# Three summed pairs per gate/up block, their shared products a block ahead and combined in PSUM

## The chip, the core and the metric

The kernel runs on one core of a Trainium2 chip. The core has TensorE (PE) for matrix products, VectorE (DVE), ScalarE (ACT) and GpSimd (POOL) for elementwise work, and SyncE (SP), whose queue issues the loads. Data lie in SBUF, matmul results in PSUM, which has eight banks of 128 x 512 float32 here. The metric is the time on the device in microseconds (us); the median of several runs counts.

## The reference

One decoder layer in float32, 256 tokens, width 2048, followed by a norm:

```
u = rmsnorm(h);  proj = u @ w_in            # 2048 x 6144
a recurrence (RG-LRU) and a retention on parts of proj give y
h = h + y @ w_out                           # 2048 x 2048
u = rmsnorm(h)
ff = silu(u @ w_ffn_gate) * (u @ w_ffn_up)  # 2048 x 5632 each
h = h + ff @ w_ffn_down                     # 5632 x 2048
out = rmsnorm(h)
```

The change lies in the line of `ff`, the gate/up stage.

## The kernel before

**Products in three matmuls.** Every float32 operand is split into a rounded high part and a remainder: `split` (L100) has ScalarE cast the source to the high part (L101) and VectorE subtract it from the source (L102). A product of 128x128 with 128x512 then takes three matmuls: high x high, high x low, low x high (L667, L668, L669).

**The gate/up stage.** The 5632 columns are taken in 11 blocks (`NB`) of 512 gate and 512 up columns, the 2048 rows in 8 steps of 256. One step of one block is a `Quad` (L592): four weight tiles of 128x512, b11 and b21 of gate, b12 and b22 of up, loaded from HBM in two halves of 512 KB. The left side, `hh[i]` (a `Left`, L518), holds the activations of the same 256 rows for two groups of 128 tokens: a11, a12 for the first, a21, a22 for the second. The four results of a block, c11 (gate, first tokens), c21 (gate, second), c12 and c22 (up), are summed over the 8 quads.

**Plain and summed quads.** A plain quad makes the eight products of `EIGHT` (L636), 24 matmuls. A quad whose number is in `SUMMED` (L32) makes the seven of `SEVEN` (L640), 21 matmuls, after Strassen and Winograd: VectorE forms t1 = b11 + b12, t2 = t1 + b22, t3 = b12 + b22, t4 = t2 + b21 (L628 to L632), and the matching left sums s1 to s4 are made once per `Left`. The products p1, p5, p6, p7 go to four banks of their own and are summed over the summed quads of the block; the other three go straight into c11, c21 and c12. After the last summed quad `post` (L723) copies p1 out and forms n = p6 - p1, then n - p5, n - p7 and a further difference in SBUF (L729, L706). When c11, c12, c21, c22 have had their last product, four VectorE instructions add these to them (L734, L736). Then come tanh (L710) and two products on VectorE (L711, L712), and two or three steps later eight transposes (`turn`, L714, L719) and two ScalarE copies put the block's result into `ff`.

**Buffers.** Raw weights: 5 tiles of 128x1024 (`raw`; the sums t1 to t4 use the same pool). Split weights: 4 tiles each for high and low (`wh`, `wl`). 58 tiles of 128x512 (`act_tile`) for the rest. PSUM: two pools of four banks, `bank` and `aux`. In `block` (L645) c11 to c22 always come from `aux`, p1 to p7 and the transposes from `bank`.

**Order.** `program` (a list) holds the steps in order: the quads they need and a function that emits the matmuls. The loop at the end emits, ahead of each step, the loads of everything up to three halves past what the step needs (`AHEAD`, L949), each with its sums and splits, then the step, then what `defer` has put off for so many steps (`tick`). The framework's planner takes the emitted order as priority, estimates when each instruction's inputs are there, and fixes an order for each engine; an instruction that is not ready by this estimate lets later ones pass. On the chip each engine follows its fixed order and waits on semaphores. Loads are all issued on SyncE's queue. The time shows no step boundaries on TensorE: matmuls of neighbouring quads are interleaved.

**Around it.** `out_post` (L545) makes each `Left` in the stage before; `norm2` (L566) makes the second norm's scale during block 0; `resid_tok` (L577) transposes the residual during blocks 1 and 2; `load_fw` runs in the last block. The down projection (`down_block`, L761) uses `block` too, in two halves of 22 quads, the last two of each as a tail.

Of the kernel before, what the change touches and what calls it, by code (L numbers as in the profile page):

```python
# [28 lines left out]

SUMMED = (2, 4)  # L32
SUMMED_DOWN = (2, 5, 8, 11, 14)


# [1 line left out]
def tile_hymba_layer(ctx: ExitStack, tc: tile.TileContext, A: dict, out: bass.AP):  # L37
    nc = tc.nc
# [29 lines left out]
    def bank(name):  # L68
        return pmm.tile([P, 512], F32, tag="mm", name=nm(name))
# [30 lines left out]
    def split(dst_h, dst_l, src):  # L100
        act.copy(out=dst_h, in_=src)  # L101
        v.tensor_tensor(out=dst_l, in0=src, in1=dst_h.bitcast(F32), op=ALU.subtract)  # L102

    class Unit:


        def __init__(self, src, pieces=1, before=None, after=None):
            self.src, self.pieces, self.before, self.after = src, pieces, before, after
# [110 lines left out]
    def defer(steps, f):  # L219
        later.append([steps, f])  # L220
# [371 lines left out]
    class Quad:  # L592

        def __init__(self, src, sums, before=None):
            self.src, self.sums, self.before = src, sums, before
# [44 lines left out]
        ("c11", "a12", "b21"), ("c21", "a22", "t4"), ("c12", "s4", "b22"),  # L642
    )

    def block(quads, lefts, post, ps, tail=(), after=None, ordered=False):  # L645
# [12 lines left out]
        def step(i):  # L658
            def run():
                while at[0] < len(todo) and todo[at[0]][0] == i:  # L660
                    m, (_, c, a, b, c0, cw, *q) = at[0], todo[at[0]]
                    if firsts[c] == m:
                        ps[c] = (aux if c in ("c11", "c12", "c21", "c22") else bank)(c)
                    q = q[0] if q else i
                    (ah, al), (bh, bl) = lefts[q][a], (t[:, c0 : c0 + cw] for t in quads[q].parts[b])
                    p, last = ps[c][:, c0 : c0 + cw], lasts[c] == m
                    pe.matmul(p, ah, bh, start=firsts[c] == m, stop=False)  # L667
                    pe.matmul(p, ah, bl, start=False, stop=False)  # L668
                    pe.matmul(p, al, bh, start=False, stop=last)  # L669
                    if last:  # L670
                        post(c)
                    at[0] += 1
                if after:
                    after(i)

            return run

        for i in range(n):
            program.append(([quads[i]], step(i)))
        if tail:  # L680
# [7 lines left out]
    def ffn_block(j):  # L688
        def after(i):
            if j == 0 and i == SUMMED[-1] + 1:  # L690
                norm2()
            if j in (1, 2) and i < 2:
                resid_tok(2 * j - 2 + i)
            if j == NB - 1 and i == 0:
                load_fw()

        ps = {}
        quads = [Quad(A["w_gu"][j * (KT // 2) + i], i in SUMMED) for i in range(KT // 2)]
        block(quads, hh, ffn_post(j, ps), ps, after=after)

    def ffn_post(j, ps):
        part = {}
# [5 lines left out]
        def gated(t):  # L708
            g, u, th = part["c21" if t else "c11"], part["c22" if t else "c12"], act_tile("th")
            act.activation(out=th, in_=g, func=AF.Tanh, scale=r2_half[:, t : t + 1])  # L710
            v.scalar_tensor_tensor(out=g, in0=th, scalar=1.0, in1=g, op0=ALU.add, op1=ALU.mult)  # L711
            v.scalar_tensor_tensor(out=g, in0=u, scalar=r2_sq[:, t : t + 1], in1=g, op0=ALU.mult, op1=ALU.mult)  # L712

        def turn(b):  # L714
            pt = bank("ft")
            for c in range(2):
                for t, g in enumerate((part["c11"], part["c21"])):
                    o = c * S + t * P
                    pe.transpose(pt[:, o : o + P], g[:, (2 * b + c) * P : (2 * b + c) * P + P], ident)  # L719
            ff[2 * j + b] = act_tile("ff")  # L720
            act.copy(out=ff[2 * j + b], in_=pt)

        def post(c):  # L723
            if c == "p1":
                part["c11"] = act_tile("c11")
                act.copy(out=part["c11"], in_=ps[c])
            elif c == "p7":
                n = act_tile("n")
                v.tensor_tensor(out=n, in0=ps["p6"], in1=part["c11"], op=ALU.subtract)  # L729
                other("c12", "c12", n, ps["p5"])  # L730
                other("c21", "c21", n, ps["p7"])
                other("c22", "c22", part["c21"], ps["p5"])
            elif c in ("c11", "c12", "c22"):
                v.tensor_tensor(out=part[c], in0=ps[c], in1=part[c], op=ALU.add)  # L734
            elif c == "c21":
                v.tensor_tensor(out=part[c], in0=ps[c], in1=part[c], op=ALU.subtract)  # L736
            if c == "c12":
                gated(0)
            if c == "c22":
                gated(1)  # L740
                defer(2, lambda: turn(0))
                defer(3, lambda: turn(1))

        return post

# [15 lines left out]
    def down_block(d):  # L761
# [188 lines left out]
    loads = [(un, j) for units, _ in program for un in units for j in range(2)]  # L950
    done, need = 0, 0
    for step, (units, run) in enumerate(program):
        need += 2 * len(units)
# [110 lines left out]
```

## Time and profile before

| | |
|---|---|
| median of 3 runs | 1105.07 us (1105.02 to 1105.36) |
| profiled execution, its own time | 1106.04 us |
| its span, first to last instruction | 1103.3 us |
| TensorE, VectorE, ScalarE busy | 99%, 80%, 56% of the span |
| gate/up stage (eleven blocks), from about | 388.5 to 872 us |
| VectorE, ScalarE busy in it | 385.3, 257.4 of 483.5 us |
| down projection, from about | 872 to 1091 us |
| read from HBM | 211.67 MB, 194 GB/s over the span |

The span is the profile's own measure from the first to the last instruction; the execution's time has what lies around it. "Busy" is the union of an engine's records. For TensorE the ends of matmuls are modelled and records of neighbours overlap, so its rate is read from start to start. An engine's idle time is put down to what ended it.

### The profile page before, as it was taken

Reading aid. Unit: us, or ns where it says so; the run is one execution under the profiler, and the core shown is the slowest. Engines: PE = TensorE matmul, PEld = TensorE weight load, DVE = VectorE, ACT = ScalarE, POOL = GpSimd, SP = SyncE. Lnnn points to the kernel's source line nnn. Section 1 sums busy time; section 2 is a strip of 40 time slices with the busy share of each in tenths; the row PEclk is TensorE's granted clock in tenths of the full one; section 3 lists DMA queues with packets and bytes.
Section 4 is the critical chain, followed back from the end, with each engine's and each line's share of the span. In section 5 each row is a group of like instructions: output and inputs, shape, how many; then the busy total and the mean of one; then the engine's idle time right before and its main releaser. Section 6 shows DMA issues by size and latency. Waiting matters only on the chain.

```text
span 1103.3 us, 14624 instructions
## 1 busy us (share of the span) xinstructions
PE 1092.4 (99%) x5328; PEld 920.5 (83%) x5328; DVE 885.3 (80%) x1249; ACT 622.1 (56%) x846; POOL 57.9 (5%) x64
## 2 busy tenths in 40 slices
PE   9999999999999999999999999999999999999996
PEld 7888888888888988888888888888888888888885
DVE  7798799978776787788787878877887999777874
ACT  7666644468665665554554545544545675554552
POOL 0602130000000000000000000000000000020001
PEclk9999999999999999999999999999999999999999
DMA  9765575554665465645746646556456465646562
GB/s 329 239 199 168 171 245 170 176 188 143 194 220 187 155 207 174 213 154 186 247 132 214 226 156 229 187 191 219 159 195 234 153 219 196 224 161 218 201 230 76
DMA packets 62215, 214.71 MB, mean 195 GB/s; under 512 B 7104, under 2 KB 7488, under 8 KB 62144
## 3 DMA queue, kind: packets, MB, share of 16 engines
q1 hardware_dynamic: 61344, 211.70, 57.6%
q0 software_dynamic: 512, 1.57, 0.5%
q8 instruction: 41, 0.67, 0.3%
q10 hardware_dynamic: 288, 0.52, 0.1%
q14 instruction: 30, 0.25, 0.1%
HBM read 211.67 MB, written 2.10 MB: 194 GB/s over the span
## 4 chain that ended last, share of the span: by engine, by line
PE 98%; DVE 0%; DMA 0%; SPq 0%; ACT 0%; issue 0%; DVEq 0%
PE c L667 18%; PE c L669 18%; PE c L668 18%; PE fm L140 16%; PE fm L141 8%; PE p L667 3%; PE p L668 3%; PE p L669 3%; PE tm L156 3%; PE tm L157 3%; PE tm L158 3%; PE ft L719 1%; DMA x<-in_x 0%; PE fm L147 0%; PE fm L145 0%; PE fm L146 0%
## 5 line engine op out<-in xcount | busy, mean ns | idle before, releaser
L102 DVE TENSOR_TENSOR wl<-raw,wh 128x1024 fp32r<-128x1024 f32 (+1 forms) x364 | 438.0, 1216 | 150.5 <-ACT wh L101 146.2
L101 ACT CAST wh<-raw 128x1024 fp32r<-128x1024 f32 (+1 forms) x364 | 371.3, 1032 | 273.7 <-PE c L669 136.9
L668 PE MATMUL c<-wl,ah 128*128 128x512 f32 x848 | 326.4, 391 | 0.0
L669 PE MATMUL c<-wh,al 128*128 128x512 f32 x848 | 325.7, 390 | 0.0
L667 PE MATMUL c<-wh,ah 128*128 128x512 f32 x848 | 286.4, 390 | 0.0
L668 PEld LDWEIGHTS c<-wl,ah 128*128 128x128 f32 x848 | 159.2, 188 | 32.8
L669 PEld LDWEIGHTS c<-wh,al 128*128 128x128 f32 x848 | 159.2, 188 | 32.7
L667 PEld LDWEIGHTS c<-wh,ah 128*128 128x128 f32 x848 | 159.1, 188 | 32.6
L140 PE MATMUL fm<-u,wh 128*128 128x512 f32 x512 | 180.1, 396 | 0.0
L141 PE MATMUL fm<-u,wl 128*128 128x256 f32 x512 | 143.9, 281 | 0.0
L101 ACT CAST wh<-sum 128x1024 fp32r<-128x1024 f32 x64 | 66.9, 1053 | 87.0 <-PE c L669 40.2
L140 PEld LDWEIGHTS fm<-u,wh 128*128 128x128 f32 x512 | 96.0, 188 | 22.1
L141 PEld LDWEIGHTS fm<-u,wl 128*128 128x128 f32 x512 | 96.7, 189 | 0.2
L102 DVE TENSOR_TENSOR wl<-sum,wh 128x1024 fp32r<-128x1024 f32 x64 | 77.1, 1224 | 3.1 <-ACT wh L101 2.4
L140 PE MATMUL fm<-y,wh 128*128 128x512 f32 x224 | 78.8, 397 | 0.0
L141 PE MATMUL fm<-y,wl 128*128 128x256 f32 x224 | 62.5, 281 | 0.0
L823 POOL TENSOR_TENSOR htok<-htok,fw 128x512 f32<-128x512 f32 (+1 forms) x7 | 10.9, 1574 | 904.8 <-ACT junk L821 904.8
L140 PEld LDWEIGHTS fm<-y,wh 128*128 128x128 f32 x224 | 41.9, 188 | 10.2
L158 PE MATMUL tm<-wh,u 128*128 128x512 f32 x128 | 48.8, 390 | 0.0
L157 PE MATMUL tm<-wl,u 128*128 128x512 f32 x128 | 48.7, 392 | 0.0
L156 PE MATMUL tm<-wh,u 128*128 128x512 f32 x128 | 46.0, 396 | 0.9 <-ACT u L277 0.9
L141 PEld LDWEIGHTS fm<-y,wl 128*128 128x128 f32 x224 | 42.3, 189 | 0.2
(246 smaller groups left out, 1231.0 us busy)
## 6 DMA issues: line engine op xcount, KB each, us to landing
raw<-in_w_gu SPq DMA_DIRECT2D x176, 512.0 KB, 5.1
raw<-in_w_down SPq DMA_DIRECT2D x88, 512.0 KB, 4.4
raw<-in_w_out SPq DMA_DIRECT2D x32, 512.0 KB, 3.7
raw<-in_w_lx SPq DMA_DIRECT2D x16, 512.0 KB, 4.7
raw<-in_w_k SPq DMA_DIRECT2D x16, 512.0 KB, 4.0
raw<-in_w_q SPq DMA_DIRECT2D x16, 512.0 KB, 4.2
raw<-in_w_rg SPq DMA_DIRECT2D x16, 512.0 KB, 3.7
raw<-in_w_lg SPq DMA_DIRECT2D x16, 512.0 KB, 4.0
```

Of the source, the lines that this page charges most:

```text
L101: act.copy(out=dst_h, in_=src)
L102: v.tensor_tensor(out=dst_l, in0=src, in1=dst_h.bitcast(F32), op=ALU.subtract)
L140: pe.matmul(ps, wh, hl, start=first, stop=False)
L141: pe.matmul(ps[:, :S], wl, hl[:, :S], start=False, stop=last)
L156: pe.matmul(ps, ah, wh, start=first, stop=False)
L157: pe.matmul(ps, ah, wl, start=False, stop=False)
L158: pe.matmul(ps, al, wh, start=False, stop=last)
L667: pe.matmul(p, ah, bh, start=firsts[c] == m, stop=False)
L668: pe.matmul(p, ah, bl, start=False, stop=False)
L669: pe.matmul(p, al, bh, start=False, stop=last)
L719: pe.transpose(pt[:, o : o + P], g[:, (2 * b + c) * P : (2 * b + c) * P + P], ident)
L823: pool.tensor_tensor(out=h, in0=h, in1=fw[cb][:, c0 : c0 + cw], op=ALU.mult)
```

## The change

Blocks 1 to 10 have three summed quads (1, 3, 5) where there were two (2, 4); block 0 keeps two, now 1 and 3. For blocks 1 to 10 the four shared products (a11 b11, s2 t2, s1 t1, s3 t3) of the three summed quads are taken out of the block and made during the block before, in three extra steps after its second, third and fourth plain quad (in block 0 after quads 4, 5 and 6). They are collected in the four banks in which c11, c12, c22, c21 of the next block will be summed. After the third, ScalarE copies c11 out and VectorE forms the differences, writing three of the four back into these banks (one of them through a ScalarE copy). The block itself begins with the other three products of each summed quad, then the five plain quads; their matmuls add onto what is in the banks. So no addition follows the last products, and tanh and the products of gate and up read PSUM.

A summed quad is loaded by two steps: `Shared` loads both halves and makes t1 to t4 (in place in its raw tiles, three instead of four), splitting t1, t2, b11, t3, and t4 into tiles that stay; `Direct` loads the second half again and splits b22, b21. The two pools of PSUM banks alternate by block (`room`), in the down projection too. The transposes of a block come five and six steps later, not two and three, but in the last block.

```diff
-SUMMED = (2, 4)
+SUMMED = (1, 3, 5)
+SUMMED_FIRST = (1, 3)
...
     def norm2():
-        ps = bank("rms")
+        ps = room(1)("rms")
...
-    def resid_tok(cb):
+    def resid_tok(cb, room):
         for t in range(2):
-            ps = bank("ht")
+            ps = room("ht")
...
+    def room(m):
+        return (aux, bank)[m % 2]
+
+    def three(p, left, right, first, last, onto=False):
+        (ah, al), (bh, bl) = left, right
+        pe.matmul(p, ah, bh, start=first, stop=False, skip_group_check=onto)
+        pe.matmul(p, ah, bl, start=False, stop=False, skip_group_check=onto)
+        pe.matmul(p, al, bh, start=False, stop=last, skip_group_check=onto)
...
-                        ps[c] = (aux if c in ("c11", "c12", "c21", "c22") else bank)(c)
+                        ps[c] = room(index + (c[0] == "p"))(c)
...
+    class Shared(Quad):
+        def load(self, half):
+            r = rpool.tile([P, 1024], F32, tag="raw", name=nm("raw"))
+            nc.sync.dma_start(out=r, in_=self.src[:, half * 1024 : half * 1024 + 1024])
+            if half == 0:
+                self.ra = r
+                return
+            ra, ta = self.ra, rpool.tile([P, 1024], F32, tag="raw", name=nm("sum"))
+            b11, b12, b22, b21 = ra[:, :512], ra[:, 512:], r[:, :512], r[:, 512:]
+            v.tensor_tensor(out=ta[:, :512], in0=b11, in1=b12, op=ALU.add)
+            v.tensor_tensor(out=ta[:, 512:], in0=ta[:, :512], in1=b22, op=ALU.add)
+            self.cut(("t1", "t2"), ta)
+            v.tensor_tensor(out=b12, in0=b12, in1=b22, op=ALU.add)
+            self.cut(("b11", "t3"), ra)
+            v.tensor_tensor(out=b21, in0=ta[:, 512:], in1=b21, op=ALU.add)
+            self.parts["t4"] = act_tile("t4h", F32R), act_tile("t4l", F32R)
+            split(*self.parts["t4"], b21)
+
+    class Direct(Quad):
+        n_loads = 1
...
+        def load(self, half):
+            r = rpool.tile([P, 1024], F32, tag="raw", name=nm("raw"))
+            nc.sync.dma_start(out=r, in_=self.src[:, 1024:2048])
+            self.cut(("b22", "b21"), r)
+            self.parts["t4"] = self.shared.parts["t4"]
...
+    def shared_steps(j):
+        ps, n = banks[j], len(SUMMED)
+        def run(m):
+            right = shared[j][m].parts
+            for c, a, b in (("c11", "a11", "b11"), ("c12", "s2", "t2"), ("c22", "s1", "t1"), ("c21", "s3", "t3")):
+                if m == 0:
+                    ps[c] = room(j)(c)
+                three(ps[c], hh[SUMMED[m]][a], right[b], m == 0, m == n - 1)
+            if m < n - 1:
+                return
+            p1, p, q = (act_tile(x) for x in ("p1", "p", "q"))
+            act.copy(out=p1, in_=ps["c11"])
+            v.tensor_tensor(out=p, in0=ps["c12"], in1=p1, op=ALU.subtract)
+            v.tensor_tensor(out=q, in0=p, in1=ps["c22"], op=ALU.subtract)
+            act.copy(out=ps["c12"], in_=q)
+            v.tensor_tensor(out=ps["c22"], in0=q, in1=ps["c21"], op=ALU.subtract)
+            v.tensor_tensor(out=ps["c21"], in0=ps["c21"], in1=p, op=ALU.subtract)
+        return [([shared[j][m]], lambda m=m: run(m)) for m in range(n)]
+
+    def gate_up(j):
+        ps, post = banks[j], ffn_post(j, banks[j])
+        ahead = shared_steps(j + 1) if j + 1 < NB else []
+        plain = [i for i in range(KT // 2) if i not in SUMMED]
+        def direct(m, quad):
+            for c, a, b in (("c11", "a12", "b21"), ("c21", "a22", "t4"), ("c12", "s4", "b22")):
+                three(ps[c], hh[SUMMED[m]][a], quad.parts[b], False, False, True)
...
+        def rest(n, quad):
+            count = {}
+            for c, a, b in EIGHT:
+                count[c] = count.get(c, 0) + 1
+                last = n == len(plain) - 1 and count[c] == 2
+                three(ps[c], hh[plain[n]][a], quad.parts[b], False, last, True)
+                if last:
+                    post(c)
+            if j in (1, 2) and n < 2:
+                resid_tok(2 * j - 2 + n, room(j + 1))
+        for m in range(len(SUMMED)):
+            quad = Direct(shared[j][m])
+            program.append(([quad], lambda m=m, quad=quad: direct(m, quad)))
+        for n, i in enumerate(plain):
+            quad = Quad(gu(j, i), False)
+            program.append(([quad], lambda n=n, quad=quad: rest(n, quad)))
+            if n and n - 1 < len(ahead):
+                program.append(ahead[n - 1])
+
+    def gate_up_first():
+        def after(i):
+            if i == SUMMED_FIRST[-1]:
                 norm2()
...
+        between = {5 - len(SUMMED) + 2 + m: [st] for m, st in enumerate(shared_steps(1))}
+        block(0, quads, hh, ffn_post(0, ps), ps, after=after, between=between)
...
+        def gate(t):
+            g, th, gated[t] = part["c21" if t else "c11"], act_tile("th"), act_tile("gated")
             act.activation(out=th, in_=g, func=AF.Tanh, scale=r2_half[:, t : t + 1])
-            v.scalar_tensor_tensor(out=g, in0=th, scalar=1.0, in1=g, op0=ALU.add, op1=ALU.mult)
+            v.scalar_tensor_tensor(out=gated[t], in0=th, scalar=1.0, in1=g, op0=ALU.add, op1=ALU.mult)
+
+        def up(t):
+            u, g = part["c22" if t else "c12"], gated[t]
             v.scalar_tensor_tensor(out=g, in0=u, scalar=r2_sq[:, t : t + 1], in1=g, op0=ALU.mult, op1=ALU.mult)
...
+            elif c[0] == "c" and c not in part:
+                part[c] = ps[c]
...
-                defer(2, lambda: turn(0))
-                defer(3, lambda: turn(1))
+                for b in range(2):
+                    defer((5 if j < NB - 1 else 2) + b, lambda b=b: turn(b))
...
-        block(quads, dl, post, ps, tail, ordered=d == 1)
+        block(NB + d, quads, dl, post, ps, tail, ordered=d == 1)
...
-    for j in range(NB):
-        ffn_block(j)
+    gate_up_first()
+    for j in range(1, NB):
+        gate_up(j)
```

More of the change, by code (lines that the diff above doesn't have):

```diff
@@ L104, in tile_hymba_layer @@
     class Unit:
+        n_loads = 2
         def __init__(self, src, pieces=1, before=None, after=None):
@@ L592, in tile_hymba_layer @@
     class Quad:
+        n_loads = 2
         def __init__(self, src, sums, before=None):
@@ L643, in tile_hymba_layer, with block @@
     )
-    def block(quads, lefts, post, ps, tail=(), after=None, ordered=False):
+    def room(m):
[5 more added lines that the diff above has]
+        pe.matmul(p, al, bh, start=False, stop=last, skip_group_check=onto)
+    def block(index, quads, lefts, post, ps, tail=(), after=None, between={}, ordered=False):
         n = len(quads) - (2 if tail else 0)
@@ L662, in run @@
                     if firsts[c] == m:
-                        ps[c] = (aux if c in ("c11", "c12", "c21", "c22") else bank)(c)
+                        ps[c] = room(index + (c[0] == "p"))(c)
                     q = q[0] if q else i
[L665 to L670, printed above, removed]
+                    right = tuple(t[:, c0 : c0 + cw] for t in quads[q].parts[b])
+                    three(ps[c][:, c0 : c0 + cw], lefts[q][a], right, firsts[c] == m, lasts[c] == m)
+                    if lasts[c] == m:
                         post(c)
@@ L679, in block @@
             program.append(([quads[i]], step(i)))
+            program.extend(between.get(i, ()))
         if tail:
@@ new lines, in tile_hymba_layer, with __init__, gu @@
+    class Direct(Quad):
+        n_loads = 1
+        def __init__(self, shared):
+            super().__init__(shared.src, True)
+            self.shared = shared
+        def load(self, half):
[3 more added lines that the diff above has]
+            self.parts["t4"] = self.shared.parts["t4"]
+    def gu(j, i):
+        return A["w_gu"][j * (KT // 2) + i]
+    banks = [{} for _ in range(NB)]
@@ new lines, in tile_hymba_layer @@
+    shared = [[Shared(gu(j, i), True) for i in SUMMED] for j in range(NB)]
+    def shared_steps(j):
[16 more added lines that the diff above has]
+        return [([shared[j][m]], lambda m=m: run(m)) for m in range(n)]
@@ L689, in after @@
+    def gate_up_first():
         def after(i):
-            if j == 0 and i == SUMMED[-1] + 1:
+            if i == SUMMED_FIRST[-1]:
                 norm2()
[L692 to L695, printed above, removed]
         ps = {}
-        quads = [Quad(A["w_gu"][j * (KT // 2) + i], i in SUMMED) for i in range(KT // 2)]
-        block(quads, hh, ffn_post(j, ps), ps, after=after)
+        quads = [Quad(gu(0, i), i in SUMMED_FIRST) for i in range(KT // 2)]
+        between = {5 - len(SUMMED) + 2 + m: [st] for m, st in enumerate(shared_steps(1))}
+        block(0, quads, hh, ffn_post(0, ps), ps, after=after, between=between)
@@ L701, in ffn_post @@
     def ffn_post(j, ps):
-        part = {}
+        part, gated = {}, [None, None]
         def other(c, name, a, b, op=ALU.subtract):
@@ L736, in post @@
                 v.tensor_tensor(out=part[c], in0=ps[c], in1=part[c], op=ALU.subtract)
-            if c == "c12":
-                gated(0)
+            if c in ("c11", "c21"):
+                gate(int(c == "c21"))
+            if c in ("c12", "c22"):
+                up(int(c == "c22"))
             if c == "c22":
-                gated(1)
-                defer(2, lambda: turn(0))
-                defer(3, lambda: turn(1))
+                for b in range(2):
+                    defer((5 if j < NB - 1 else 2) + b, lambda b=b: turn(b))
         return post
@@ L949, in tile_hymba_layer @@
     AHEAD = 3
-    loads = [(un, j) for units, _ in program for un in units for j in range(2)]
+    loads = [(un, j) for units, _ in program for un in units for j in range(un.n_loads)]
     done, need = 0, 0
     for step, (units, run) in enumerate(program):
-        need += 2 * len(units)
+        need += sum(un.n_loads for un in units)
         while done < min(len(loads), need + AHEAD):
```

9 lines of the change are left out of this document (4 added, 5 removed).

## The prediction

> **What bounds the kernel now.** I read the page first: its span, its engine shares and its chain.
>
> ```profile
> span 1103.3 us, 14624 instructions
> PE 1092.4 (99%) x5328; PEld 920.5 (83%) x5328; DVE 885.3 (80%) x1249; ACT 622.1 (56%) x846; POOL 57.9 (5%) x64
> PE 98%; DVE 0%; DMA 0%; SPq 0%; ACT 0%; issue 0%; DVEq 0%
> ```
>
> The chain that ended last runs on TensorE for 98% of the span. VectorE (DVE) is busy for 80%, so it is second, and it is the engine that this change loads.
>
> "Busy" for TensorE says little, since the ends of matmuls are modelled. So I asked which waits TensorE had; the answer has two lines, both from the first microseconds. Then I read its timeline for the start-to-start time.
>
> ```profile
> PE warm L94 <- DVE eps_t L87: 1.0, 1, 1.0
> PE tm L156 <- ACT u L277: 0.9, 1, 0.9
> ...
> 878.01 1.07 PE L668 MATMUL c<-wl,ah 128*128 128x512 f32 x4
> 878.92 1.07 PE L669 MATMUL c<-wh,al 128*128 128x512 f32 x4
> 879.83 1.07 PE L667 MATMUL c<-wh,ah 128*128 128x512 f32 x4
> ```
>
> Four matmuls start every 0.907 us, so one 512-column matmul costs 0.2267 us of the path; the 1.07 only contains the modelled tail. A gate/up block repeats itself every 43.14 us, as these pieces of the chain, one from each of three blocks, show:
>
> ```profile
> 704.05 0.91 PE c L667 x4
> ...
> 747.18 0.91 PE c L667 x4
> ...
> 790.32 0.91 PE c L667 x4
> ```
>
> The program gives a block 6 plain quads of 24 matmuls and 2 summed ones of 21, 186 in all: 186 x 0.2267 = 42.17 us, and 0.97 us is left for the eight transposes of the block. So these blocks are a solid row of matmuls without a hole. A matmul removed is 0.2267 us gained; every hole that the change makes is lost in full.
>
> How much cover VectorE has is read from one block's window, from the costs of single instructions, and from its timeline.
>
> ```profile
> 690.00:733.00 43.00, 43.00 (x195) 35.55 (x194) 34.28 (x41) 22.61 (x25) 0.00 (x0) 1.00 0.58 196
> ...
> L102 DVE TENSOR_TENSOR wl<-raw,wh 128x1024 fp32r<-128x1024 f32 x348 | 427.0, 1241 | 149.2 <-ACT wh L101 144.9 <-PE fm L141 2.3
> L628 DVE TENSOR_TENSOR sum<-raw 128x512 f32<-128x512 f32 x32 | 22.0, 688 | 18.7 <-DMA raw<-in_w_gu 15.6 <-DMA raw<-in_w_down 3.1
> L734 DVE TENSOR_TENSOR c<-c,c 128x512 f32<-128x512 f32 x33 | 22.6, 686 | 0.0
> ...
> 721.50 1.23 DVE L102 TENSOR_TENSOR wl<-raw,wh 128x1024 fp32r<-128x1024 f32 x1 [0.73 <-ACT wh L101]
> 726.25 2.36 DVE L102 TENSOR_TENSOR wl<-raw,wh 128x1024 fp32r<-128x1024 f32 x2 [3.53 <-ACT wh L101]
> 728.53 0.68 DVE L734 TENSOR_TENSOR c<-c,c 128x512 f32<-128x512 f32 x1
> 729.13 0.68 DVE L736 TENSOR_TENSOR c<-c,c 128x512 f32<-128x512 f32 x1
> ```
>
> The window's third pair is VectorE: 34.28 of 43.00 us. A 128x512 instruction has a record of 0.69 us, but the next one starts 0.60 us after it (728.53, 729.13); two 128x1024 ones take 2.36 and one 1.23, so the start-to-start time is 1.13. I use 0.60 and 1.13. By program order a block has 12 + 6 subtractions of split halves at 1.13, 2 at 0.60 (b11), 8 sums at 0.60 and 12 instructions behind the products at 0.60: 20.3 + 1.2 + 4.8 + 7.2 = 33.5 us, against 34.28 measured.
>
> **The removed matmuls.** Blocks 1 to 10 get three summed quads in place of two, so each has 183 matmuls; block 0 keeps two. That is 30 x 0.2267 = 6.80 us off a path that has nothing else on it. Transposes, residual tiles, the first two projections, the down projection and the tail keep their matmuls. A steady block should be 43.14 - 0.68 = 42.46 us long.
>
> **VectorE in a steady block.** A plain quad costs 2 x 1.13 = 2.26 us. A summed quad is now split over two steps, Shared (four sums, two 1024-wide subtractions, t4's: 2.4 + 2.26 + 0.6 = 5.26) and Direct (1.13), which is 6.39 together, as before. The combination is four instructions instead of four, but no additions follow the last products; four of gate and up are left. Sum: 5 x 2.26 + 3 x 6.39 + 2.4 + 2.4 = 35.3 us; scaled by 34.28/33.5 it is 36.1 of 42.46, or 85% against 80%. ScalarE does the casts and one more copy:
>
> ```profile
> 725.17 2.00 ACT L101 CAST wh<-raw 128x1024 fp32r<-128x1024 f32 x2 [3.71 <-PE c L669]
> L101 ACT CAST wh<-raw 128x1024 fp32r<-128x1024 f32 x348 | 361.5, 1052 | 271.0 <-PE c L669 136.9 <-PE fm L140 47.4 <-issue 26.4
> L721 ACT COPY ff<-ft 128x512 f32<-128x512 f32 x22 | 12.8, 584 | 11.6 <-PE ft L719 11.6
> ```
>
> A summed quad has 3 x 1.0 + 0.6 of casts where a plain one has 2.0, so ScalarE rises by 1.6 and a copy of 0.58, from 22.61 to about 24.8 of 42.46. Neither engine becomes the bound on the mean.
>
> **Where it is tight.** The load is uneven. With R a plain step (24 x 0.2267 = 5.44 us), S a Shared step (2.72) and D a Direct step (2.04), a block runs D D D R R S R S R S R. From the end of the second R to the next block's first D, TensorE has 3 S + 3 R = 24.5 us. In it VectorE must do the splits of three R (6.8), two S (10.5; the first S is ready by then), the combination (2.4) and the split for D (1.13): 20.8, or 23.2 with gate and up, which D doesn't need. It fits, with 1.3 to 3.7 us to spare. In the rest of the block, 17 us of D and R, VectorE has 14.5 us of work with the first S. What eats the reserve is waiting, and this is where the block before shows it (columns: us in total, times, longest; four blocks):
>
> ```profile
> ACT wh L101 <- PE c L669: 53.9, 29, 3.8
> DVE wl L102 <- ACT wh L101: 27.0, 17, 3.5
> ...
> DVE sum L628 <- DMA raw<-in_w_gu: 7.6, 4, 2.4
> ```
>
> ScalarE waits mostly for TensorE to free a split buffer (four of wh, four of wl), and VectorE for ScalarE: they are held up by TensorE, not the reverse. I put this at nothing to 0.2 us a block, 1 us in all.
>
> **The combination** stands between the last S and the first D, and R covers it with 5.44 us. Its chain is p1's copy 0.58, p 0.69, q 0.69, then c12's copy 0.58 beside c22 and c21, 1.3: 3.3 us; without that cover it would cost 33 us in ten blocks. No instruction of VectorE or ScalarE writes PSUM in this trace. Bounds for such a write: the 0.58 and 0.60 of the rows that read PSUM (nothing excludes somewhat less, which the cover would hide), and 1.23, the row of twice the width. I take the lower, since L734 with one operand in PSUM costs 686 ns, as L628 does with none (688); with the upper, three writes add 1.9 us and the chain is 5.2, still under 5.44, but with no room for other work in the queue. A matmul that adds onto such a bank is of the same kind as those that collect now: 0.2267; with the dearest mean of a matmul's row, 417 ns for p1's against 390, 9 a block would add 0.24 us, 2.4 in all.
>
> ```profile
> L667 PE MATMUL p<-bh,ah 128*128 128x512 f32 x32 | 13.3, 417 | 0.0
> ```
>
> **DMA.** A summed quad's second half is loaded again: 19 loads a block for 16, that is 196 x 19/16 x 43.14/42.46 = 236 GB/s, and 4 x 0.524 MB in 8.16 us = 257 GB/s in the R S stretch.
>
> ```profile
> GB/s 173 261 227 103 153 302 174 162 162 282 89 175 278 237 93 159 312 138 175 232 247 105 156 286 192 174 176 300 66 182 289 203 153 164 312 68 175 280 240 66
> ...
> raw<-in_w_gu SPq DMA_DIRECT2D x169, 512.0 KB, 5.1
> ```
>
> Slices of the gate/up stage reach 312 GB/s, so the rate is to be had. All loads stand in SyncE's one queue, in program order; behind a load that waits for one of five raw buffers stand the next R's loads. A Shared quad holds three raw buffers where the summed one held four, which pays for the shorter distance. Cost: nothing, while S is prepared before the R in front of it is done; past that, up to the 2.4 us of the longest wait for a load above.
>
> **Block 0 and the odd ones.** Block 0 has 186 + 36 matmuls, 50.3 us (the 36 are taken out of block 1's share, so the total is the same), and 33.5 + 3 x 5.26 + 2.4 = 51.7 us of VectorE. Its first four quads give VectorE 20.4 us for 17.3; from there to the last S it has 25.0 us of work in 24.5. So it enters the tight part 3 us ahead and ends about even: 0 to 2 us, I take 0.5. In blocks 1 and 2 the residual transposes use the same four banks as the next block's products, each freed by a ScalarE copy of 0.58: 0.3 us in two blocks. One more left side is summed in the stage before (four instructions of 0.29 and one of 0.69, under 2 us of VectorE, busy for 64 of 88.5), hidden by its matmuls:
>
> ```profile
> L532 DVE TENSOR_TENSOR s<-ff 128x128 f32<-128x128 f32 x5 | 1.5, 292 | 0.0
> 300.00:388.50 88.50, 88.50 (x527) 78.08 (x526) 63.97 (x98) 53.73 (x90) 0.00 (x0) 1.00 0.57 185
> ```
>
> The other banks in the down projection change no order of its matmuls and free no wait, as TensorE has none there: nothing.
>
> **The sum.** The profiled execution took 1106.04 us, of it 1103.3 span and 2.7 around it. 1106.04 - 6.80 + 1.0 + 0.5 + 0.3 = 1101.0. The median of the runs is 1105.07, 0.97 below that execution, so the forecast is 1100.0 us.
>
> **Rivals.** *The split buffers make holes, slower.* With four buffers, an R behind an S can be prepared only when the R before that S is done, and S gives just 2.72 us. The cast takes 1.05 and the subtraction 1.23, so its first half is ready after 2.3, the second after 3.4; TensorE wants them after 2.72 and, in written order, 3.40. One 128x512 instruction ahead of them in VectorE's queue (0.60) makes a hole of 0.2 to 0.6. There are 30 such places, so the gain of 6.80 is gone at 0.23 us each, and at 0.6 the time is 1105.07 - 6.8 + 18 = 1116.3. For it: S leaves VectorE sums of its own to do just there. Against it: the planner may take the first half's products first, which moves the second half's time to 5.4 us, and this trace has like places (b22, b21 of a summed quad, one buffer in 2.72 us) without a wait of TensorE.
>
> *VectorE gets its full records, slower.* If instructions that write PSUM or read it in new places don't overlap, each costs 0.69 and 1.23: the stretch of 24.5 us then needs 3 x 2.46 + 2 x 5.91 + 2.76 + 1.23 = 23.2, and 26.0 with gate and up. If those come first, ten blocks lose 1.5 us each: 1105.07 - 6.8 + 15 = 1113.3. Against it stand the 0.60 above, two instructions that read PSUM. The Trainium skill, "VectorE: DVE Perf Modes", section "The DRAIN you can't avoid", says the next vector instruction doesn't start until the pipe is empty, and adds that one that is not held starts earlier; the trace agrees with the addition: 0.60 between starts where a record has 0.69.
>
> *The combination is late, no change.* If VectorE does the fourth R's subtractions and gate before p and q, the chain of 3.3 us gets 2 to 3 us longer and passes 5.44 by about 0.6 us a block: 1105.07 - 6.8 + 6 = 1104.3. Against it: it is written before them, and D's three first matmuls need c11 alone.
>
> **How the numbers follow.** Forecast 0.68; split buffers 0.14; full records 0.04; late combination 0.14. About 0.2%, 2.2 us, is what a measurement of this kernel can tell from no change: faster 0.68, same 0.14, slower 0.18. The forecast's own range is 1098.2 (no hole) to 1102.8. The whole range goes from 1098.0 to 1110, which takes in the late combination and the slower cases to a hole of 0.39 us at each of the 30 places; what is beyond has a chance of about 0.1.
>
> **What would show it.** Right: 5298 matmuls; a repeat of 42.5 us in blocks 3 to 9; VectorE near 36 us of each; no waits of TensorE for wl, wh or c. The split buffers would show as TensorE waiting for L102's wl at the R behind an S; the combination as waits for the copy into c12 or c21's subtraction ahead of D; full records as 0.69 between starts. I am wrong if the repeat is 43 us or more, or if block 0 loses over 2 us.

## The result and the profile after

The changed kernel takes 1136.72 us (median; 1134.16 to 1141.13 in four runs) against 1105.21 us: the ratio is 1.0289, 95% interval 1.0256 to 1.0323. It is 31.5 us slower, where 1100.0 was forecast. The page of its profiled execution (1135.66 us) begins:

```profile
span 1133.9 us, 14754 instructions
PE 1100.2 (97%) x5298; PEld 915.2 (81%) x5298; DVE 906.6 (80%) x1274; ACT 639.0 (56%) x877; POOL 57.4 (5%) x64
PE 60%; DVE 18%; DMA 15%; issue 4%; ACT 2%; DVEq 0%; SPq 0%; ACTq 0%
```

The 30 matmuls are gone (5298). VectorE's share is what it was. But the chain that ended last runs on TensorE for 60% of the span, not 98%: a third of it is now VectorE and loads. One block of the steady part, in the view by windows (third pair VectorE, fourth ScalarE, last number GB/s):

```profile
726.40:774.00 47.60, 43.91 (x192) 34.78 (x191) 36.26 (x43) 24.16 (x28) 0.00 (x0) 1.00 0.63 210
```

From the first transpose of one block to that of the next, the ten distances are 42.2, 42.7, 45.4, 49.4, 45.9, 47.0, 47.7, 46.0, 46.5 and, in the last block, which makes nothing ahead, 30.0 us. The block before the change took 43.14. The first two look like the forecast's 42.46, but they hold 172 and 171 matmuls, where a block has 183, and the residual's transposes, so they don't bear it out; those from the fifth to the ninth, with 183 each, are 3.4 to 5.2 us longer than forecast. From the gate/up stage on (388.5 us), adding up every distance between starts of TensorE's matmuls of over 0.33 us, less 0.227, gives 34.5 us of holes in 79 places; by the same count the kernel before has none there.

A small part of this is the clock. From 623.9 us, right behind holes of 0.6, 1.0 and 0.9 us, the clock granted to TensorE is half for 3.4 us:

```profile
623.90:627.30 3.40, 3.40 (x10) 2.63 (x9) 3.40 (x6) 1.91 (x3) 0.00 (x0) 0.51 0.66 219
```

Matmuls start every 0.427 us there in place of 0.227, which makes them about 1.5 us longer in all, part of the 34.5; the distance of 49.4 us contains this stretch. The kernel before has no such stretch until its last matmuls are done.

What stands in the chain of this block, and in which order:

```profile
by line: DMA raw<-in_w_gu 39.7%; DVE wl L103 27.4%; issue 10.8%; DVE raw L721 4.0%; DVE sum L717 3.0%; DVE sum L716 3.0%; DVE raw L719 2.7%; DVE gated L821 2.5%; ACT wh L102 2.2%; DVE c L765 1.5%; DVE q L762 1.4%; DVE gated L825 1.4%; DVE t
...
741.95 7.26 DMA raw<-in_w_gu
749.91 1.22 DVE wl L103
752.34 2.28 DVE wl L103 x2
754.63 6.89 DMA raw<-in_w_gu
761.63 1.06 ACT wh L102
```

There is no TensorE in it. A load is issued at 741.95 and lands 7.26 us later; sums and subtractions follow; the one that ends at 754.62 frees a raw tile, and the next load of the chain is issued at 754.63. From issue to issue these are 12.68 us. VectorE's timeline in the same stretch shows what waits, and where it comes in its queue:

```profile
748.03 0.69 DVE L716 TENSOR_TENSOR sum<-raw 128x512 f32<-128x512 f32 x1 [3.24 <-DMA raw<-in_w_gu]
749.30 0.69 DVE L717 TENSOR_TENSOR sum<-sum,raw 128x512 f32<-128x512 f32 x1 [0.58 <-DMA raw<-in_w_gu]
749.91 1.22 DVE L103 TENSOR_TENSOR wl<-raw,wh 128x1024 fp32r<-128x1024 f32 x1
751.05 0.69 DVE L719 TENSOR_TENSOR raw<-raw,raw 128x512 f32<-128x512 f32 x1
751.65 0.69 DVE L721 TENSOR_TENSOR raw<-sum,raw 128x512 f32<-128x512 f32 x1
```

The sum t1 (L716) waits 3.24 us for its load, and TensorE then stands 0.88 us at 751.2 for a cast behind these sums:

```profile
745.21 1.05 ACT L102 CAST wh<-raw 128x1024 fp32r<-128x1024 f32 x1 [1.67 <-DMA raw<-in_w_gu]
...
751.20 0.74 PE L659 MATMUL c<-wh,sh 128*128 128x512 f32 x2 [0.88 <-ACT wh L102]
```

The first of these lines shows that the loop isn't the loads' alone. By the order of casts and subtractions this cast belongs to the subtraction at 749.91. It had ended at 746.26, while VectorE stood idle; but t1 and t2 come first in VectorE's order. Run in that idle time, the subtraction would have taken an estimated 1.1 us off the loop of 12.68 us, and the load that was issued at 751.16, when it freed its tile, could have gone up to 3.6 us sooner. That is theory B of the next section, inside the loop of theory A.

The waits of before and after over the same stretch, from 600 to 820 us (total, times, longest), show the turn. Before:

```profile
ACT wh L101 <- PE c L669: 71.9, 39, 3.8
DVE sum L628 <- DMA raw<-in_w_gu: 8.3, 5, 2.4
ACT wh L101 <- DMA raw<-in_w_gu: 5.5, 10, 2.1
```

After:

```profile
ACT wh L102 <- DMA raw<-in_w_gu: 36.8, 26, 3.2
ACT wh L102 <- DVE sum L717: 32.1, 8, 5.2
DVE sum L716 <- DMA raw<-in_w_gu: 25.0, 9, 3.9
PEld c L660 <- DVE wl L103: 14.6, 13, 1.7
ACT wh L102 <- PE c L661: 10.4, 6, 4.4
```

Before, ScalarE waited for TensorE to free split buffers (71.9 us), which is what a TensorE that never lacks work looks like. After, it waits for loads and for the sum t2 (L717), which comes behind them, and TensorE waits for splits. SyncE's own waits don't show the turn: it waited for VectorE to free a raw tile for 182 of these 220 us before and for 178 after, so a pool without a free tile is no sign by itself.

### The profile page after: what moved, and what is told of

Its sections match the earlier page's. It is cut to its first block, busy times and chain, and to the rows that moved or that the text cites. A ratio compares the mean times of both kernels' runs of the same rounds, so it can differ in the third digit from the quotient of the medians.

```text
span 1133.9 us, 14754 instructions
## 1 busy us (share of the span) xinstructions
PE 1100.2 (97%) x5298; PEld 915.2 (81%) x5298; DVE 906.6 (80%) x1274; ACT 639.0 (56%) x877; POOL 57.4 (5%) x64
## 4 chain that ended last, share of the span: by engine, by line
PE 60%; DVE 18%; DMA 15%; issue 4%; ACT 2%; DVEq 0%; SPq 0%; ACTq 0%
PE fm L143 15%; DMA raw<-in_w_gu 15%; DVE wl L103 10%; PE c L660 9%; PE c L661 8%; PE c L659 8%; PE fm L144 8%; PE tm L159 3%; PE tm L160 3%; PE tm L161 3%; ACT wh L102 2%; DVE raw L721 1%; DVE sum L717 1%; DVE raw L719 1%; PE p L659 1%
## 5 line engine op out<-in xcount | busy, mean ns | idle before, releaser
L103 DVE TENSOR_TENSOR wl<-raw,wh 128x1024 fp32r<-128x1024 f32 (+1 forms) x384 | 461.6, 1217 | 112.9 <-ACT wh L102 108.4
L102 ACT CAST wh<-raw 128x1024 fp32r<-128x1024 f32 (+1 forms) x384 | 390.4, 1032 | 274.2 <-DMA raw<-in_w_gu 60.3
L660 PE MATMUL c<-wl,ah 128*128 128x512 f32 x788 | 309.8, 395 | 14.8 <-DVE wl L103 14.7
L661 PE MATMUL c<-wh,al 128*128 128x512 f32 x788 | 306.7, 391 | 0.0
L659 PE MATMUL c<-wh,ah 128*128 128x512 f32 x788 | 261.4, 393 | 1.4 <-ACT wh L102 1.4
L103 DVE TENSOR_TENSOR wl<-sum,wh 128x1024 fp32r<-128x1024 f32 x54 | 65.3, 1222 | 6.4 <-ACT wh L102 6.2
L659 PE MATMUL c<-wh,sh 128*128 128x512 f32 x132 | 49.8, 403 | 5.8 <-ACT wh L102 5.5
L716 DVE TENSOR_TENSOR sum<-raw 128x512 f32<-128x512 f32 x30 | 20.7, 691 | 42.9 <-DMA raw<-in_w_gu 42.9
L660 PE MATMUL c<-wl,sh 128*128 128x512 f32 x132 | 52.1, 395 | 0.0
L661 PE MATMUL c<-wh,sl 128*128 128x512 f32 x132 | 52.0, 394 | 0.0
```

Of the source, the lines that this page charges most:

```text
L659: pe.matmul(p, ah, bh, start=first, stop=False, skip_group_check=onto)
L660: pe.matmul(p, ah, bl, start=False, stop=False, skip_group_check=onto)
L661: pe.matmul(p, al, bh, start=False, stop=last, skip_group_check=onto)
L716: v.tensor_tensor(out=ta[:, :512], in0=b11, in1=b12, op=ALU.add)
```

## The experiments

Theories: **A**, the five raw tiles, that is the loop of load, sums, split and the next load into the freed tile; **B**, VectorE's own order and latency; **C**, the rate of the loads; **D**, the combining in PSUM; **E**, the split buffers (the forecast's first rival). Times are medians; ratios to the kernel before have 95% intervals.

**One raw tile more.**

```diff
-rpool = ... tc.tile_pool(name="raw", bufs=5)
+rpool = ... tc.tile_pool(name="raw", bufs=6)     # acts 58 -> 57, late 5 -> 4
```

> The changed kernel with six raw weight tiles instead of five (one tile of the late pool, of which four of five are used, and one of the 58 small tiles pay for it). Theory A, the raw tiles: a load can be issued only when VectorE's subtraction has freed a tile, takes about 5 us to land, and the next split waits for it; a sixth tile lets one more load be under way, so the repeat of a gate/up block falls from about 46.7 us to 44 or less and the time to 1105 to 1118. Rival B, VectorE's own order and latency: a raw tile more changes nothing, above 1130. Rival C, the rate of the loads (19 a block for 16): little, 1128 or more.

Measured: 1120.02 us, 1.0134 (1.0104 to 1.0163). Half of the loss is back with one tile of 512 KB. It is 2 us outside what A had named; B and C are further off.

**The second load left out.** Direct steps split a resident tile, the same weights in every block (a small tile and one of the late pool pay for it).

```diff
-nc.sync.dma_start(out=r, in_=self.src[:, 1024:2048])
-self.cut(("b22", "b21"), r)
+self.cut(("b22", "b21"), still[0])
```

> The changed kernel, with the second load of b22 and b21 left out: each Direct step splits one resident tile that is loaded once, so all Direct steps use the same weights; casts, subtractions and matmuls are as many as in the changed kernel. Takes away 30 loads and 30 uses of a raw tile. Theory A: three of 22 uses of raw tiles a block fall away, but none in the stretch of Shared and plain steps: a part comes back, 1110 to 1125. Rival C, the rate of the loads: 16 loads a block as before, so nearly all comes back, 1100 to 1105. Rival B: nothing, above 1130.

Measured: 1113.70 us, 1.0076 (1.0047 to 1.0106). 23 of the 31.5 us come back, so the second load costs much, both as a load and as a use of a tile. It isn't the rate alone: with 16 loads a block, as before the change, 8.5 us remain.

**Two pairs in the new way.**

```diff
-SUMMED = (1, 3, 5)
+SUMMED = (1, 3)
```

> The changed kernel with two summed pairs in every block (1 and 3) instead of three: the shared products are still made a block ahead and combined in PSUM, the transposes come a step sooner because a block has one step less. 186 matmuls a block as before the change, 18 loads a block, 20 uses of raw tiles (the kernel before: 20, the changed one: 22). Theory A: the stretch with Shared steps is 8 us shorter and the raw tiles nearly suffice: 1104 to 1112. Rival D, the way of combining in PSUM itself makes the holes: 20 us or more remain, above 1125.

Measured: 1113.92 us, 1.0074 (1.0051 to 1.0097); repeats of 43.7 to 43.9 us in all steady blocks but one, against 43.14 before the change. 22.8 of the 31.5 us hang on the third pair. A missed its bound by 2 us; D's 20 us are not there.

**Another order of the steps.**

```diff
-D D D R R S R S R S R
+D R D S R R S D R S R
```

> The changed kernel with the steps of a block in another order, D R D S R R S D R S R instead of D D D R R S R S R S R (both pairs of residual tiles and the transposes of the block before come a little sooner so that the banks are free). Same instructions, same loads, five raw tiles; only the distance between Shared steps changes, from 8.2 us to 10 to 15. Theory A: the loop of the raw tiles is asked for less at its worst and most of the loss comes back, 1102 to 1118. Rival C: the mean rate is the same, no change, 1130 or more. Rival B: a part, since VectorE's load is evened too, 1115 to 1130.

Measured: 1154.99 us, 1.0450 (1.0420 to 1.0480). It is 18 us slower still; A and B missed, and C, whose "1130 or more" holds the number, had said no change. I had looked at the distance between Shared steps and overlooked that a Direct step now stands next to a Shared one: three loads in 12 + 9 matmuls, 3 x 0.524 MB in 4.76 us or 330 GB/s, where Shared and plain steps ask for 257. VectorE waited 47.4 us at t1 between 600 and 820 us against 25.0:

```profile
DVE sum L716 <- DMA raw<-in_w_gu: 47.4, 14, 5.3
ACT wh L102 <- DMA raw<-in_w_gu: 32.0, 27, 3.1
PEld c L660 <- DVE wl L103: 24.0, 15, 4.0
```

This fits a demand over a few microseconds, but doesn't show it: the run moved the transposes and the residual tiles too. And part of the 18 us may be the clock: this trace has six stretches of 3.4 us at half the granted clock, each behind a hole of 2.4 to 3.8 us, where the changed kernel's has one. In them the matmuls take about 9 us longer, against 1.5.

**Two raw tiles more.**

```diff
-rpool = ... tc.tile_pool(name="raw", bufs=5)
+rpool = ... tc.tile_pool(name="raw", bufs=7)     # acts 58 -> 55, late 5 -> 4
```

> The changed kernel with seven raw tiles (55 small tiles for 58, four of the late pool for five). Theory A, the raw tiles: six gave 1120.0 from 1136.7; a seventh brings the remaining holes down again, to 1099 to 1110. Rival E, what remained at six is the order of the split buffers (R behind S, the forecast's first rival): no further gain, 1116 to 1122.

Measured: 1107.76 us, 1.0019 (1.0003 to 1.0036). The chain between 640 and 770 us, and three blocks in a row:

```profile
by line: PE c L659 32.8%; PE c L660 32.7%; PE c L661 32.6%; PE ft L832 2.0%
...
687.30:729.70 42.40, 42.40 (x193) 35.20 (x192) 36.89 (x44) 23.89 (x28) 0.00 (x0) 1.00 0.70 241
729.70:772.10 42.40, 42.40 (x193) 35.20 (x192) 35.94 (x43) 23.88 (x28) 0.00 (x0) 1.00 0.69 233
772.10:814.50 42.40, 42.40 (x192) 35.20 (x192) 36.67 (x43) 23.88 (x28) 0.00 (x0) 1.00 0.69 239
```

The steady block is on TensorE again, at 42.40 us, with 19 loads and 233 to 241 GB/s. That settles C (the rate is to be had) and D (the combining makes no hole). It doesn't settle B, as the order on VectorE is another one with seven tiles. Left are 9.0 us of holes: 5.6 in the first blocks (500 to 600 us), 3.3 in the down projection.

**Seven raw tiles, three split buffers.**

```diff
-rpool = ... bufs=5;  wpool = ... bufs=4
+rpool = ... bufs=7;  wpool = ... bufs=3          # acts 58, late 5
```

> Seven raw tiles, paid for by the split buffers: three pairs of wh and wl in place of four (58 small tiles as before). Theory A alone: like seven raw tiles with four split buffers. Rival E: a plain step needs two split buffers at once, so with three only one can be prepared ahead; holes at every step, well above the run with four, 1150 or more. What lies between the two runs is the price of one split buffer.

Measured: 1136.06 us, 1.0278 (1.0246 to 1.0309). Neither range holds it. With one pair of split buffers fewer beside seven raw tiles the kernel is 28 us slower. ScalarE's wait for TensorE to free one is 82.3 us between 600 and 820 us, and 58.7 with four:

```profile
ACT wh L102 <- PE c L661: 82.3, 50, 2.6
```

In the changed kernel itself this wait was 10.4. So the split buffers weren't what the changed kernel ran into; one pair fewer, and they are.

**Two pairs, seven raw tiles.** The edits of the two runs together.

> Two summed pairs a block in the new way (186 matmuls a block, as before the change) with seven raw tiles. Theory A: the 9 us that two pairs lost with five raw tiles are the same loop of loads and go: 1104 to 1107, no gain, since no matmul is saved. Rival D, combining in PSUM a block ahead has a price of its own: 1110 or more.

Measured: 1109.74 us, 1.0039 (1.0024 to 1.0054). The loss halves, to 4.7 us. Neither bound is met; since three pairs run without a hole at 42.40, it is not a price of combining. The profiled execution, the slowest of six, has 7.2 us of holes from the first gate/up block to the down projection, nearly all at waits for a split; what makes these late isn't settled.

**Three pairs in the old way.**

```diff
-SUMMED = (2, 4)
+SUMMED = (2, 4, 6)      # in the kernel before; norm2 stays after quad 5
```

> The kernel before with three summed pairs (2, 4, 6) in the old way, in all blocks: 183 matmuls a block, 16 loads, four raw tiles a summed quad; nothing a block ahead and nothing written into PSUM. 33 matmuls fewer are 7.5 us. Theory A: 22 uses of raw tiles a block as in the changed kernel, four at once in a summed quad, but a summed quad of 21 matmuls gives 4.8 us for them instead of 2.7 and loads its second half once; a part of the gain is lost, 1098 to 1112. If the third pair costs VectorE or the raw tiles as much in the old way, 1125 or more.

Measured: 1124.38 us, 1.0172 (1.0143 to 1.0202), at the edge of the second case. The third pair alone, with no second load and nothing written to PSUM, loses 19 us, again with waits for loads (between 600 and 820 us, at the cast of b11 and at t1):

```profile
ACT bh L101 <- DMA raw<-in_w_gu: 30.6, 10, 5.7
DVE sum L628 <- DMA raw<-in_w_gu: 24.5, 12, 4.0
```

**Six raw tiles and one for t1 and t2.** Space comes from tables that are not used after attention.

```diff
+late.append(ctx.enter_context(tc.tile_pool(name="sums", bufs=1)))
-ra, ta = self.ra, rpool.tile([P, 1024], F32, tag="raw", ...)
+ra, ta = self.ra, late[1].tile([P, 1024], F32, tag="sum", ...)
```

> The changed kernel with six raw tiles and, from the gate/up stage on, one tile more for t1 and t2 alone (cr and sr, the tables of the rotary step, are given up after the attention stage, and one unused tile of the late pool); 57 small tiles. Theory A: in gate/up as good as seven raw tiles, a repeat of 42.4 us. With seven raw tiles 9.2 us of holes were left, 5.6 in blocks 1 to 3 and 3.3 in the down projection, where 55 small tiles may be short. If so, 57 bring the second part back: 1101 to 1106. If the holes in the down projection come from the order of the loads, 1105 to 1109.

Measured: 1104.67 us, 0.9995 (0.9986 to 1.0005). No difference from the kernel before; repeats of 42.4 us in the steady blocks, 3.7 us of holes in the profiled execution, 2.6 of them in the down projection.

**One summed quad in block 0.**

```diff
-SUMMED_FIRST = (1, 3)
+SUMMED_FIRST = (3,)     # with the buffers of the run before
```

> As the run with six raw tiles and a sum tile, with one summed quad in block 0 (3) instead of two (1 and 3): 3 matmuls more, 0.7 us, and some 4 us less of VectorE in block 0, which also makes the shared products of block 1. If the holes of blocks 1 to 3 come from a late start out of block 0, they shrink, and the time is 1 to 4 us below that run; if they come from the residual transposes in blocks 1 and 2, it is 0.7 us above.

Measured: 1103.78 us, 0.9985 (0.9976 to 0.9994): a little faster than the kernel before. From the run with two it is 0.9 us away and the intervals overlap, so what block 0 does isn't decided.

**Three pairs in the old way with these buffers.** The sum tile and six raw tiles in the kernel before with pairs 2, 4, 6.

> Three summed pairs in the old way (2, 4, 6 in all blocks; 183 matmuls a block, no second load) with the six raw tiles and the sum tile, also in the down projection. 33 matmuls fewer than before, 7.5 us. Theory A: its 24 us of holes with five raw tiles are the same loop of loads and go for the most part: 1099 to 1107. If VectorE's twelve instructions behind the products, or the split buffers (three a summed quad), limit it, 1110 or more.

Measured: 1111.37 us, 1.0048 (1.0031 to 1.0065). 13 of its 19 us come back. With the same buffers the new way is 6.7 us better (1104.67): VectorE has 38.58 us of a 43.00 us window there, against 36.25 of 42.40 in the new way, and TensorE's longest wait in total is for its additions behind the last products.

```profile
PE c L669 <- DVE c L736: 3.3, 9, 1.3
...
690.00:733.00 43.00, 42.75 (x193) 35.11 (x192) 38.58 (x48) 24.03 (x28) 0.00 (x0) 1.00 0.59 196
```

**All 58 small tiles.** As the run with one summed quad in block 0, with space from five instead of eight temporary tiles in attention.

> The changed kernel with six raw tiles and a sum tile, one summed quad in block 0, and all 58 small tiles (paid for by five instead of eight temporary tiles in the attention stage and by giving up r1 and the first sum of squares after it). If the 2 to 3 us of holes that were left in the down projection come from 57 small tiles, they go and the time is 1100.5 to 1102.5; if they come from the order of loads, 1102.5 to 1105; if the temporary tiles make holes in the attention stage, above 1105.

Measured: 1103.49 us, 0.9984 (0.9975 to 0.9993), the same as with 57. So the holes in the down projection don't come from the small tiles; there, too, VectorE waits for loads ahead of a first sum, in this run at 990 and 1004 us:

```profile
989.99 0.69 DVE L638 TENSOR_TENSOR sum<-raw 128x512 f32<-128x512 f32 x1 [2.65 <-DMA raw<-in_w_down]
...
1004.45 0.69 DVE L638 TENSOR_TENSOR sum<-raw 128x512 f32<-128x512 f32 x1 [4.54 <-DMA raw<-in_w_down]
```

**The buffers without the change.** The kernel before with six raw tiles, the sum tile and 57 small tiles.

> The kernel before, unchanged but for the same buffers as the run with six raw tiles and a sum tile (57 small tiles). Theory A: TensorE has no holes in it, so more raw tiles can give nothing: 1104.5 to 1107 (holes in the down projection may come with 57 small tiles). If raw tiles alone were worth something, below 1103.

Measured: 1119.68 us, 1.0131 (1.0117 to 1.0145), 14.5 us slower. I had expected nothing. With other buffers the planner makes another order, and in it VectorE comes to a sum before its load has landed, with the splits and additions of the block behind it in its queue:

```profile
643.76 0.69 DVE L630 TENSOR_TENSOR sum<-raw 128x512 f32<-128x512 f32 x1 [3.00 <-DMA raw<-in_w_gu]
645.17 0.69 DVE L631 TENSOR_TENSOR sum<-sum,raw 128x512 f32<-128x512 f32 x1 [0.72 <-DMA raw<-in_w_gu]
645.78 2.35 DVE L102 TENSOR_TENSOR wl<-raw,wh 128x1024 fp32r<-128x1024 f32 x2
648.05 0.68 DVE L736 TENSOR_TENSOR c<-c,c 128x512 f32<-128x512 f32 x1
```

So tiles alone give the kernel before nothing, and the gain of the variants against it is not the buffers' own. But it also means that each run with another number of tiles changed the order as well. How much of 1136.7, 1120.0 and 1107.8 is tiles (A) and how much the order planned with them (B) stays open: no run changes the one without the other, and none changes `AHEAD`, which sets how early a load is emitted.

## Why the prediction was wrong, point by point

**What bounds the kernel and what a matmul costs: right.** 30 matmuls at 0.2267 us are gone; where the blocks run without holes (seven raw tiles) the repeat is 42.40 us, forecast 42.46.

**VectorE and ScalarE in a steady block: right.** Forecast 36.1 and 24.8 us; measured 36.26 and 24.16 in the changed kernel, 35.94 to 36.89 and 23.9 with seven raw tiles. The mean load wasn't the trouble.

**The combination: right.** Over the whole kernel TensorE waited 1.0 us for c21's subtraction and 0.3 for c12's copy. The writes into PSUM cost what the lower bound said:

```profile
L764 DVE TENSOR_TENSOR c<-q,c 128x512 f32<-128x512 f32 x10 | 6.9, 691 | 0.1
L763 ACT COPY c<-q 128x512 f32<-128x512 f32 x10 | 5.9, 590 | 0.2
```

**The loads: this step failed.** It said "Cost: nothing, while S is prepared before the R in front of it is done", and that three raw tiles where there had been four "pays for the shorter distance". Neither was worked out, and the sum has no term for it, though the text named a price past that condition, up to 2.4 us. What came instead is 34.5 us of holes, and loads on the chain. The sum took the loads as a rate (236 and 257 GB/s against slices of 312), and the rate was indeed no bound. What I didn't count is how long a tile is held. A plain step uses 2 tiles and a Shared step 3, five uses in 8.16 us, with five tiles: each may be held for 8.16 us on average. From the rows that I had quoted, 5.1 us to landing, sums at 0.60, a cast of 1.05 and a subtraction of 1.13, a plain use needs an estimated 7.3 us and the three of a Shared step 8.5, 8.1 and 3.4 (the last, for t1 and t2, has no load): 6.9 on average, which leaves about 1.2 us a use for every wait. In the trace after, 12.68 us pass from an issue to the next one in the chain, 7.26 of them to landing. The condition in my sentence was the whole question. A sign of it was visible before: t1 waited up to 2.4 us for its load in blocks with two summed quads, 24 + 21 matmuls or 10.2 us apart.

That loads stand on the path is shown by the chain; the runs without the second load and without the third pair, which give back 23.0 and 22.8 us, agree. That the hold of a tile is the reason, rather than the order planned for VectorE, is argued: more tiles bring the time back, but each such run has another order, and in the loop above both are at work.

The Trainium skill, "DMA: Bandwidth & Descriptors", section "Latency and other measured facts", puts the fixed cost of a transfer at about 2 us. Here a 512 KB load took 3.1 us at the least and 5.0 at the median (changed kernel, 604 to 820 us), 1.9 us more. The four that were issued at 739.08, 740.21, 740.82 and 741.95 landed after 3.3, 4.9, 7.1 and 7.3 us, and the one issued at 751.16, 6.3 us behind the last before it, after 3.5: what comes on top of the least goes with loads issued shortly before.

**The first rival, the split buffers:** right in sign, in that TensorE waits for wl, and wrong in cause. Had it been so, ScalarE's wait for TensorE would have grown; it fell from 71.9 to 10.4 us. **Full records:** no; the next start is still 0.60 behind the instructions that read and write PSUM (L764 at 765.58, L765 at 766.18, the next at 766.78). **A late combination:** no, by the two waits above. The case that happened was not among the rivals, and 1136.7 lies far beyond the upper end of 1110.

**Block 0 and the first blocks:** forecast 0.8 us of holes. With seven raw tiles, where the steady blocks have none, blocks 1 to 3 have 5.6, so this term was too small as well. In the changed kernel block 0 itself has 3.5 us of holes (408 to 441 us); with seven raw tiles it has none, so the loads or the order did this too, and not VectorE's load.

**What would show it:** the list named a repeat of 43 us or more, or over 2 us lost in block 0, as the sign of being wrong; both came. It had no sign for loads.

## What to carry to other kernels

When a stage runs without holes, ask of every buffer pool on its feed how many uses an interval has and how long one use is held, from the issue of the load to the instruction that frees the tile; the rate of the loads and the mean load of an engine don't answer that. Do this for the densest few microseconds of the new order, not for the block, and look at what stands behind a waiting instruction in its engine's order. And where a planner fixes the order, another number of buffers is another order: it can cost more than the buffer gives, and a run of the old kernel with the new buffers tells the two effects apart only in part.

## What the runs showed of the hardware that was not expected

Landing times of the 512 KB loads hardly differ whether the loads are on the path or not: 3.1, 5.0, 7.8 us (least, median, most) in the changed kernel, 3.1, 4.9, 7.7 with seven raw tiles and 3.1, 5.1, 6.7 before, between 604 and 820 us. Holes may cost more than their own length: in four of the traces with holes (the changed kernel, six raw tiles, the other order, three split buffers) the granted clock falls to half for 3.4 us behind some of them, and matmuls then start every 0.427 us in place of 0.227. Not every hole has this behind it, with seven raw tiles none of up to 2.0 us, and what decides it isn't shown. The time also varies more from run to run: 1134.2 to 1141.1 us in the changed kernel and 1105.1 to 1111.8 with seven raw tiles, against 1104.9 to 1107.3 for the kernel before over all rounds; no run shows why.
